# Retention's and GLA's q and k projected for all four heads at once

## The chip, the cores and the metric

One NeuronCore of a Trainium2 chip runs the whole program as one launch. The metric is the device time of one execution in microseconds. The time before is 2238.5 us, the median of three runs (2236.98 to 2249.15).

## The reference, cut to what matters

One layer of a hybrid decoder for 256 prompt tokens and 8 x 4 sample tokens, 288 tokens in all, width 2048, float32:

```
h = rmsnorm(x);  P = h @ w_in            # one projection, columns split among the mixers
retention (4 heads, dk 128, dv 256): rotary q, k; chunked recurrence; group norm; swish gate
gated DeltaNet "GDN" (8 heads, 128 x 128): conv + SiLU on q, k, v; delta rule; gated norm
GLA (4 heads, dk 128, dv 256): per-channel forget gate; chunked recurrence; gated norm
merge = sum_i sigmoid(P_gate_i) * (branch_i @ w_branch[i]);  x += merge @ w_o
x += SwiGLU(rmsnorm(x));  y = rmsnorm(x)
outputs: y and the new states of every head, for the prompt and for each sample row
```

The columns of `w_in` hold, among others, retention's q (512 columns, 128 per head), its k (512), its v (1024) and its gate (1024), and the same four for GLA.

## The kernel before, in words

Every product is taken in three parts: an activation is split into a high and a low float32r half (`xh`, `xl`), a weight likewise (`wh`, `wl`), and TensorE adds wh*xh, wh*xl and wl*xh into PSUM. Each weight tile is therefore loaded (`raw`, 512 KB, four buffers), cast by ScalarE (`wh`) and subtracted by VectorE (`wl`), with four buffers of each, before TensorE uses it. The weights stand still in TensorE and the 288 tokens stream through.

Two routines do this for the mixers. `products` (L405, called by `x_in`) takes 256 columns at a time and loads four blocks of 128 rows per tile, so that a row of a transfer has 256 columns; L422 and L423 are its cast and subtraction. `halves` (L337, called by `x_halves`) takes 512 columns, loads two blocks of rows per tile and works through the two halves of the columns in turn, with four PSUM accumulators (`pd`); its cast is at L355. With `perm`, which rotary needs, the cast reads even and odd columns apart.

The mixers' stage is a loop of four turns (L1457). Each turn first projects a pair of GDN heads (`gdn`: q, k, v with a short convolution, and a gate `sz`, four calls of `x_in`), then a pair of retention heads (first two turns) or of GLA heads (last two): q and k by `x_in`, two heads' v and gate by `x_halves` (`two_heads`). The heads' own work (scores, triangular solve, states, norms) is written as generators: `gdn_mix` for a pair of GDN heads, `ret_head` and `gla_head` for one wide head. A generator is started when its inputs are projected. `pump` is called after each pair of row blocks of a projection and steps every active generator by its rate, the GDN kind in one call and the others in the next, so that the heads' small instructions come in between the products in program order. A scheduler then orders each engine's queue in a simulated run, the older instruction first, with loads, casts and subtractions of weights ahead of the rest.

Buffers: `ev` (nine tiles of two heads x 288) holds projected q, k, v and gates; `s0` (three tiles of 4 KB per partition) holds the sample states, of which a GDN head takes one and a wide head two; `srow` (one) holds the old convolution rows of a GDN block and `ns` (one) the new ones on their way out. All these transfers are issued by SyncE (SP), in one queue with the weight loads. The GDN pool is freed when the last pair is done; the pool of the following branch stage (gates of the merge, branch products, `yr`, `bt`) is made after it and uses memory that it frees.

Of the kernel before, what the change touches and what calls it, by code (L numbers as in the profile page):

```python
# [10 lines left out]
F32 = mybir.dt.float32  # L11
F32R = mybir.dt.float32r
# [27 lines left out]
R1 = 4  # L40
R2 = 6
EV = 9
ORDER = (1, 2, 3, 0)

O_RQ, O_RK, O_RV, O_RG = 0, 512, 1024, 2048
O_GQ, O_GK, O_GV = 3072, 4096, 5120
# [55 lines left out]
class Trunk:  # L102
# [231 lines left out]
            evict(m, tiles[m][:, :T])  # L334
        return pool

    def halves(self, xh, xl, wv, kt, evict):  # L337


        nc, tc = self.nc, self.tc  # L340
        acc = [self.t(self.pd, (P, 512), "pd") for _ in range(4)]
        for k0 in range(0, kt, 4):
            raws = []
            for z in (k0, k0 + 2):
                raw = self.t(self.wp, (P, 2, WIDE), "raw", bufs=4)
                with tc.high_priority():
                    nc.sync.dma_start(out=raw, in_=wv[:, z:z + 2])
                raws.append(raw)
            for half in range(2):
                for z, raw in enumerate(raws):  # L350
                    wh = self.t(self.wp, (P, 2, CHUNK), "wh", F32R, bufs=4)
                    wl = self.t(self.wp, (P, 2, CHUNK), "wl", F32R, bufs=4)
                    src = raw[:, :, half * CHUNK:(half + 1) * CHUNK]
                    with tc.high_priority():
                        nc.scalar.copy(wh, src)  # L355
                        self.tt(wl, src, wh.bitcast(F32), ALU.subtract)
                    for k in range(2):
                        kk = k0 + 2 * z + k
                        for m in range(2):
                            ms = slice(m * P, (m + 1) * P)  # L360
                            o = acc[2 * half + m][:, :T]
                            self.mm(o, wh[:, k, ms], xh[kk], kk == 0, False)
                            self.mm(o, wh[:, k, ms], xl[kk], False, False)
                            self.mm(o, wl[:, k, ms], xh[kk], False, kk == kt - 1)
                        self.pump(k)
                if k0 + 4 == kt:
                    for m in range(2):
                        evict(2 * half + m, acc[2 * half + m][:, :T])

    def x_halves(self, c0, evict):  # L370
        self.halves(blocks(self.xh), blocks(self.xl), self.w_in(c0, WIDE), KT, evict)

    def products4(self, xh, xl, wv, kt, steps=None):
        nc, tc = self.nc, self.tc
# [179 lines left out]
    def gdn_conv(self, pair, part):  # L554

        nc, m = self.nc, self.mx
        c0 = part * 1024 + pair * CHUNK
        b0 = c0 // P
        cat = self.t(self.gd, (P, 2, CA), "cat", bufs=2)
        nc.vector.memset(cat[:, :, 0:3], 0.0)  # L560
        srow = self.t(self.gd, (24, CHUNK), "srow", bufs=1)
        nc.sync.dma_start(out=srow, in_=self.i["state_gdn_conv"][0].rearrange("b r c -> (b r) c")[:, c0:c0 + CHUNK])
        smp = [cat[:, mm_, 3 + NPR:CW].rearrange("p (b r) -> p b r", r=7) for mm_ in range(2)]
        out = self.t(m, (P, 2, T), "ev", bufs=EV)

        def ev(mm_, pp):
            self.tt(cat[:, mm_, 3:3 + NPR], pp[:, :NPR], self.rb[:, :NPR], ALU.mult)
            self.tt(smp[mm_][:, :, 3:7], pp[:, NPR:].rearrange("p (b t) -> p b t", t=NT),
                    self.rb[:, NPR:].rearrange("p (b t) -> p b t", t=NT), ALU.mult)

        self.x_in(O_GQ + c0, ev)
        pt = self.ps()
        for mm_ in range(2):
            self.tr(pt[:, 24 * mm_:24 * mm_ + 24], srow[:, mm_ * P:(mm_ + 1) * P])
# [12 lines left out]
        l3 = self.t(self.gd, (P, 2, 27), "l3", bufs=2)  # L587
        for mm_ in range(2):
            nc.vector.tensor_copy(l3[:, mm_].rearrange("p (b r) -> p b r", r=3),
                                  cat[:, mm_, NPR:NPR + 63].rearrange("p (b r) -> p b r", r=7)[:, :, 0:3])  # L590
        self.start(self.conv_state(l3, c0), 1, "conv")
        return out

    def conv_state(self, l3, c0):
        nc = self.nc
        yield
        yield
        pt = self.ps()
# [4 lines left out]
        nc.sync.dma_start(out=self.o["p_conv"][0, 0, :, c0:c0 + CHUNK], in_=ns[0:3])  # L603
        nc.sync.dma_start(out=self.o["s_conv"][0].rearrange("b r c -> (b r) c")[:, c0:c0 + CHUNK], in_=ns[3:27])

    def gated(self, n, c0):

# [43 lines left out]
    def gdn_mix(self, pair, qs, ks, vs, szs):  # L651
# [58 lines left out]
        for hh, z in enumerate(hd):  # L710
# [14 lines left out]
            dts = []  # L725
            for g, (t0, w) in enumerate(GROUPS):
                nmk = self.mats[:, MAT_NM] if g < 2 else self.small[:, SM_NM:SM_NM + 32]
                dt_ = big("dt", 3, w)
                self.stt(dt_, cb[:w, t0:t0 + w], gcol[:w, g, h:h + 1], nmk, ALU.subtract, ALU.add)
                self.act(dt_, dt_, AF.Exp)  # L730
                dts.append(dt_)
# [206 lines left out]

    def expand(self, v3, e, b0):
        n = 512 // e  # L940
        vx = self.t(self.mx, (3 * NS, 512), "vx", F32R, bufs=3)
        self.nc.gpsimd.tensor_tensor(vx.rearrange("p (b e) -> p b e", e=e), v3.unsqueeze(1).to_broadcast([3 * NS, n, e]),
                                     self.bmask[:, b0:b0 + n].unsqueeze(2).to_broadcast([3 * NS, n, e]), op=ALU.mult)
        return vx
# [13 lines left out]
    def gdn(self, pair):  # L958
# [3 lines left out]
            self.gates()  # L962
        v = self.gdn_conv(pair, 2)
        sz = self.gated(2, O_DZ + pair * CHUNK)
        self.start(self.gdn_mix(pair, q, k, v, sz), 1, "gdn")


    def values(self, v):
# [13 lines left out]
    def wide_head(self, h, st, st2, vt, vs, zq, kd, s0, state_out, p_out, decay, sg, gcols, n):  # L982
# [3 lines left out]

        def halves(b):
            sh = self.t(m, (P, 256), "sh", F32R, bufs=2)
            sl = self.t(m, (P, 256), "sl", F32R, bufs=4)
            src = s0[b // 4][:, b % 4]  # L990
            nc.scalar.copy(sh, src)
            nc.gpsimd.tensor_tensor(sl, src, sh.bitcast(F32), op=ALU.subtract)
# [81 lines left out]
            s0.append(s)  # L1074
        return s0

    def evict_scaled(self, c0, perm=False):
        out = self.t(self.mx, (P, 2, T), "ev", bufs=EV)

        def ev(m, pp):  # L1080
            self.tt(out[:, m], pp, self.rb, ALU.mult)

        self.x_in(c0, ev, perm)
        return out


    def rotated(self, c0):
        out = self.t(self.mx, (P, 2, T), "ev", bufs=EV)

        def ev(m, pp):  # L1090
            b = self.r1()
            self.tt(b[0:64], pp[64:128], self.rot[64:128, 1], ALU.mult)
            self.tt(b[64:128], pp[0:64], self.rot[0:64, 1], ALU.mult)
            self.tt(out[:, m], pp, self.rot[:, 0], ALU.mult)
            self.tt(out[:, m], out[:, m], b, ALU.add)

        self.x_in(c0, ev, perm=True)
        return out

    def spread(self, h, q, f):  # L1100
# [69 lines left out]
        yield from self.wide_head(h, st, st2, vt, vs, zq, kd, s0, s_out, p_out, lambda b: g4, sg, None, 0)  # L1170

    def ret(self, pair):
        q = self.rotated(O_RQ + pair * CHUNK)
        k = self.rotated(O_RK + pair * CHUNK)
        self.two_heads(O_RV + pair * WIDE, O_RG + pair * WIDE,
                       lambda hh, v, sg: self.ret_head(2 * pair + hh, q[:, hh], k[:, hh], v, sg), "ret")

# [99 lines left out]
    def gla(self, pair):  # L1277
        b = self.t(self.mx, (P, 2, T), "ev", bufs=EV)
        self.nc.sync.dma_start(out=b, in_=self.fsum[pair])
        q = self.t(self.mx, (P, 2, T), "ev", bufs=EV)  # L1280

        def evq(m, pp):
            self.stt(q[:, m], pp, DK ** -0.5, self.rb, ALU.mult, ALU.mult)

        self.x_in(O_LQ + pair * CHUNK, evq)
        k = self.evict_scaled(O_LK + pair * CHUNK)
        self.two_heads(O_LV + pair * WIDE, O_LG + pair * WIDE,
                       lambda hh, v, sg: self.gla_head(2 * pair + hh, q[:, hh], k[:, hh], v, sg, b[:, hh]), "gla")

# [159 lines left out]
    def run(self):  # L1449
# [4 lines left out]
        self.wd = self.pool("wide", stack=mst, side="right")  # L1454
        self.gd = self.pool("gdn", stack=dst, side="right")
        self.gdn_setup()
        for n, (f, pair) in enumerate(((self.ret, 1), (self.ret, 0), (self.gla, 1), (self.gla, 0))):  # L1457
            self.gdn(ORDER[n])
            if n == 0:
                self.wide_setup()  # L1460
# [66 lines left out]
```

## Time and profile before

| what | value |
|---|---|
| time, median of 3 runs | 2238.5 us |
| profiled execution | 2237.24 us, span 2235.4 us |
| TensorE matmul busy | 2170.1 us, 97% |
| VectorE, ScalarE, GpSimd busy | 1356.0, 1027.8, 213.5 us |
| HBM read, written | 341.70 MB, 25.69 MB |

A busy time counts an engine's instructions, not its waits. The clock column of a window is the share of TensorE's full clock that was granted there. A wait is put down to the instruction or transfer that ended it. The mixers' stage lasts from the start to about 765 us, the branch stage follows.

### The profile page before, as it was taken

The page shows a single profiled execution, that of the slowest core. Times are in us where ns is not written, and L with a number is a line of the kernel's source. Part 1 is how long each engine was busy: PE and PEld are TensorE (multiplying, and loading weights), DVE is VectorE, ACT ScalarE, POOL GpSimd, SP SyncE. Part 2 cuts the span into 40 slices and gives each one's busy share as a digit, 9 for nine tenths or more (in the row PEclk, how much of TensorE's full clock was granted, in tenths as well). Part 3 has the DMA queues.
Part 4 walks back from the last instruction along what each step waited for, and adds up shares of the span by engine and source line. Part 5 has one row for each costly group of instructions (what it writes and reads, how often), then busy time and mean ns, then how long its engine had stood idle before and what let it go on. Part 6 is the DMA issues. An engine that isn't in the chain of part 4 may idle for free.

```text
span 2235.4 us, 43857 instructions
## 1 busy us (share of the span) xinstructions
PE 2170.1 (97%) x17020; PEld 2113.2 (95%) x17020; DVE 1356.0 (61%) x2952; ACT 1027.8 (46%) x2114; POOL 213.5 (10%) x264
## 2 busy tenths in 40 slices
PE   8999989999989999999999999999999999999997
PEld 7899979989878999999999999999999999999997
DVE  6776765685777586555565655565555445556544
ACT  5645443453445355444444444444444334444443
POOL 2103301241233042000000000000000000000000
PEclk9999999999999999999999999999999999999998
DMA  8747876864997666677666566655555555555553
GB/s 221 160 127 164 148 161 121 192 176 124 132 114 189 125 192 199 190 194 186 175 187 168 163 191 179 179 167 167 164 169 163 169 164 167 167 164 169 161 160 118
DMA packets 251511, 370.23 MB, mean 166 GB/s; under 512 B 20318, under 2 KB 120248, under 8 KB 251144
## 3 DMA queue, kind: packets, MB, share of 16 engines
q1 hardware_dynamic: 250136, 364.66, 63.7%
q8 instruction: 133, 2.18, 0.4%
q0 software_dynamic: 896, 2.45, 0.3%
q14 instruction: 74, 0.61, 0.1%
q10 hardware_dynamic: 272, 0.34, 0.1%
HBM read 341.70 MB, written 25.69 MB: 164 GB/s over the span
## 4 chain that ended last, share of the span: by engine, by line
PE 87%; DMA 9%; DVE 2%; ACT 1%; issue 1%; POOL 0%; SPq 0%; POOLq 0%; DVEq 0%; ACTq 0%
PE pd L129 54%; PE pm L129 32%; DMA raw<-in_w_in_dram 4%; DMA yr<-ys 1%; PE pm L126 1%; DMA out_dram<-s 1%; DVE wl L135 1%; DMA srow<-in_state_gdn_conv_dram 1%; DVE r L144 0%; DMA ev<-fsum 0%; DMA s<-in_state_ret_dram 0%; DMA xa<-in_x_prompt_dram 0%; ACT wh L422 0%; DMA xb<-in_x_sample_dram 0%; DMA out_dram<-ns 0%
## 5 line engine op out<-in xcount | busy, mean ns | idle before, releaser
L135 DVE TENSOR_TENSOR wl<-raw,wh 128x512 fp32r<-128x512 f32 (+1 forms) x1208 | 846.2, 703 | 705.0 <-ACT wh L386 489.7
L129 PE MATMUL pd<-xh,wh 128*128 128x288 f32 x2768 | 824.4, 300 | 16.2 <-ACT wh L422 12.3
L129 PE MATMUL pd<-xl,wh 128*128 128x288 f32 x2768 | 824.5, 299 | 0.0
L129 PE MATMUL pd<-xh,wl 128*128 128x288 f32 x2768 | 816.9, 299 | 1.0 <-DVE wl L135 1.0
L386 ACT CAST wh<-raw 128x512 fp32r<-128x512 f32 x784 | 485.2, 620 | 643.9 <-PE pd L129 331.6
L129 PEld LDWEIGHTS pd<-xh,wh 128*128 128x128 f32 x2768 | 523.4, 189 | 21.8 <-ACT wh L422 13.1
L129 PEld LDWEIGHTS pd<-xl,wh 128*128 128x128 f32 x2768 | 524.2, 189 | 3.7 <-issue 1.6
L129 PEld LDWEIGHTS pd<-xh,wl 128*128 128x128 f32 x2768 | 520.5, 189 | 5.6 <-DVE wl L135 2.9
L355 ACT CAST wh<-raw 128x512 fp32r<-128x512 f32 x224 | 138.0, 618 | 194.3 <-PE pd L129 178.6
L129 PE MATMUL pm<-xh,wl 128*128 128x288 f32 x704 | 207.8, 295 | 0.0
L129 PE MATMUL pm<-xl,wh 128*128 128x288 f32 x704 | 207.3, 294 | 0.0
L129 PE MATMUL pm<-xh,wh 128*128 128x288 f32 x704 | 207.0, 294 | 0.0
L422 ACT CAST wh<-raw 128x512 fp32r<-128x512 f32 x192 | 117.8, 622 | 101.3 <-PE pd L129 52.9
L129 PEld LDWEIGHTS pm<-xh,wh 128*128 128x128 f32 x704 | 132.1, 188 | 0.0
L129 PEld LDWEIGHTS pm<-xl,wh 128*128 128x128 f32 x704 | 132.1, 188 | 0.0
L129 PEld LDWEIGHTS pm<-xh,wl 128*128 128x128 f32 x704 | 132.0, 188 | 0.0
L129 PE MATMUL pd<-ah,wl 128*128 128x288 f32 x352 | 103.9, 295 | 0.0
L129 PE MATMUL pm<-ah,wl 128*128 128x288 f32 x352 | 103.9, 295 | 0.0
L129 PE MATMUL pm<-al,wh 128*128 128x288 f32 x352 | 103.8, 295 | 0.0
L129 PE MATMUL pd<-al,wh 128*128 128x288 f32 x352 | 103.7, 295 | 0.0
L129 PE MATMUL pm<-ah,wh 128*128 128x288 f32 x352 | 103.7, 295 | 0.0
L129 PE MATMUL pd<-ah,wh 128*128 128x288 f32 x352 | 103.6, 294 | 0.0
(372 smaller groups left out, 2927.9 us busy)
## 6 DMA issues: line engine op xcount, KB each, us to landing
raw<-in_w_in_dram SPq DMA_DIRECT2D x252, 512.0 KB
raw<-in_w_gate_up_dram SPq DMA_DIRECT2D x176, 512.0 KB
raw<-in_w_down_dram SPq DMA_DIRECT2D x88, 512.0 KB
raw<-in_w_branch_dram SPq DMA_DIRECT2D x48, 512.0 KB
raw<-in_w_o_dram SPq DMA_DIRECT2D x32, 512.0 KB
out_dram<-s SPq DMA_DIRECT2D x16, 512.0 KB
s<-in_state_gdn_dram SPq DMA_DIRECT2D x8, 512.0 KB
s<-in_state_ret_dram SPq DMA_DIRECT2D x16, 256.0 KB
```

The source lines that it names most:

```text
L126: self.nc.tensor.transpose(out, in_, self.ident[:k, :k])
L129: self.nc.tensor.matmul(out, lhsT=lhsT, rhs=rhs, start=start, stop=stop)
L135: self.nc.vector.tensor_tensor(out, a, b, op=op)
L355: nc.scalar.copy(wh, src)
L386: nc.scalar.copy(wh, raw[:, k])
L422: nc.scalar.copy(h, src)
```

## The change

Retention and GLA project q and k of all four heads in the turn of pair 0, by `x_halves` in rows of 512 columns; pair 0's come into `ev` tiles, pair 1's into two new tiles `qk`, which pair 1's turn takes. So pair 0 comes first now, in both, and the order of the GDN pairs is another one. `halves` learns `perm`, with the cast and the subtraction of such a tile done in two pieces, one for each block of rows. Four kinds of buffers get one fewer (`l3`, `dt`, `vx`, `sl`). The load of `srow` and the two stores of `ns` are issued by ScalarE. The last GDN pair's generator is stepped twice per pump.

```diff
-ORDER = (1, 2, 3, 0)
+ORDER = (1, 0, 2, 3)
...
-    def halves(self, xh, xl, wv, kt, evict):
+    def halves(self, xh, xl, wv, kt, evict, perm=False):
...
+                    pieces = [(wh, wl, src)]
+                    if perm:
+                        src = src.rearrange("p k (h m two) -> p k h two m", two=2, h=2)
+                        h, l = (y.rearrange("p k (h two m) -> p k h two m", two=2, h=2) for y in (wh, wl))
+                        pieces = [(h[:, y], l[:, y], src[:, y]) for y in range(2)]
                     with tc.high_priority():
-                        nc.scalar.copy(wh, src)
-                        self.tt(wl, src, wh.bitcast(F32), ALU.subtract)
+                        for h, l, src in pieces:
+                            nc.scalar.copy(h, src)
+                            self.tt(l, src, h.bitcast(F32), ALU.subtract)
...
+    def both(self):
+        return self.t(self.mx, (P, 2, T), "ev", bufs=EV), self.t(self.mx, (P, 2, T), "qk", bufs=2)
...
-        nc.sync.dma_start(out=srow, in_=self.i["state_gdn_conv"][0]...)
+        nc.scalar.dma_start(out=srow, in_=self.i["state_gdn_conv"][0]...)
...
-        l3 = self.t(self.gd, (P, 2, 27), "l3", bufs=2)
+        l3 = self.t(self.gd, (P, 2, 27), "l3", bufs=1)
...
-        nc.sync.dma_start(out=self.o["p_conv"]..., in_=ns[0:3])
-        nc.sync.dma_start(out=self.o["s_conv"]..., in_=ns[3:27])
+        nc.scalar.dma_start(out=self.o["p_conv"]..., in_=ns[0:3])
+        nc.scalar.dma_start(out=self.o["s_conv"]..., in_=ns[3:27])
...
-                dt_ = big("dt", 3, w)
+                dt_ = big("dt", 2, w)
...
-        vx = self.t(self.mx, (3 * NS, 512), "vx", F32R, bufs=3)
+        vx = self.t(self.mx, (3 * NS, 512), "vx", F32R, bufs=2)
...
-        self.start(self.gdn_mix(pair, q, k, v, sz), 1, "gdn")
+        self.start(self.gdn_mix(pair, q, k, v, sz), 2 if pair == ORDER[-1] else 1, "gdn")
...
-            sl = self.t(m, (P, 256), "sl", F32R, bufs=4)
+            sl = self.t(m, (P, 256), "sl", F32R, bufs=3)
...
     def rotated(self, c0):
-        out = self.t(self.mx, (P, 2, T), "ev", bufs=EV)
+        out = self.both()
...
-        self.x_in(c0, ev, perm=True)
+        self.x_halves(c0, ev, perm=True)
...
     def ret(self, pair):
-        q = self.rotated(O_RQ + pair * CHUNK)
-        k = self.rotated(O_RK + pair * CHUNK)
+        if pair == 0:
+            self.qk = self.rotated(O_RQ), self.rotated(O_RK)
+        q, k = (z[pair] for z in self.qk)
...
     def gla(self, pair):
-        self.x_in(O_LQ + pair * CHUNK, evq)
-        k = self.evict_scaled(O_LK + pair * CHUNK)
+        if pair == 0:
+            qs = self.both()
...
+            self.x_halves(O_LQ, evq)
+            ks = self.both()
...
+            self.x_halves(O_LK, evk)
+            self.qk = qs, ks
+        q, k = (z[pair] for z in self.qk)
...
-        for n, (f, pair) in enumerate(((self.ret, 1), (self.ret, 0), (self.gla, 1), (self.gla, 0))):
+        for n, (f, pair) in enumerate(((self.ret, 0), (self.ret, 1), (self.gla, 0), (self.gla, 1))):
```

## Rows read from the trace of the kernel before

**Rows 1.** The page, part 1: busy us (share) x instructions of each engine.
```profile
PE 2170.1 (97%) x17020; PEld 2113.2 (95%) x17020; DVE 1356.0 (61%) x2952; ACT 1027.8 (46%) x2114; POOL 213.5 (10%) x264
```

**Rows 2.** The chain in order of time: start, us, what; one block of 512 columns.
```profile
1401.92 25.44 PE pm L129 x192
```

**Rows 3.** Windows of the mixer stages: busy us of each engine, clock, DMA share, GB/s.
```profile
core 0: us, PE busy (x) PEld busy (x) DVE busy (x) ACT busy (x) POOL busy (x), PEclk, DMA share, GB/s
...
50.00:75.00 25.00, 17.65 (x119) 16.91 (x118) 15.90 (x39) 10.32 (x24) 3.67 (x4) 0.86 0.90 190
...
275.00:300.00 25.00, 15.09 (x98) 13.62 (x96) 8.21 (x30) 8.71 (x32) 2.61 (x3) 0.90 0.86 187
300.00:325.00 25.00, 25.00 (x197) 23.86 (x196) 23.74 (x79) 13.23 (x32) 1.42 (x2) 0.90 0.61 125
...
475.00:500.00 25.00, 21.15 (x133) 19.07 (x132) 21.77 (x82) 14.90 (x53) 8.67 (x10) 0.80 0.70 210
...
575.00:650.00 75.00, 69.69 (x515) 64.76 (x514) 54.10 (x154) 34.53 (x89) 24.04 (x36) 0.98 1.01 139
650.00:675.00 25.00, 13.97 (x95) 12.72 (x94) 15.29 (x34) 8.45 (x24) 6.65 (x7) 0.84 0.86 137
```

**Rows 4.** The same view, four microseconds after a stall.
```profile
484.00:488.00 4.00, 4.00 (x18) 4.00 (x18) 3.79 (x24) 2.61 (x9) 1.01 (x1) 0.50 1.00 325
```

**Rows 5.** SP's queue in order of time: start, us of the issue, line, transfer.
```profile
50.56 0.41 SPq L562 DMA_DIRECT2D srow<-in_state_gdn_conv_dram  x1
```

**Rows 6.** TensorE in order of time: start, us, out<-in, [idle before <- what ended it].
```profile
5.29 0.20 PE L126 MATMUL pm<-ident,rm 16*128 16x16 f32 x1 [0.47 <-DMA rm<-in_norm_mix_dram]
...
58.58 0.41 PE L126 MATMUL pm<-ident,srow 24*128 24x24 f32 x2 [6.49 <-DMA srow<-in_state_gdn_conv_dram]
...
284.49 0.58 PE L129 MATMUL pd<-xh,wh 128*128 128x288 f32 x1 [4.50 <-ACT wh L422]
```

**Rows 7.** ScalarE in order of time, its queue of issues (ACTq) included.
```profile
1.20 0.45 ACTq L188 DMA_DIRECT2D rm<-in_norm_mix_dram  x1
...
283.53 0.36 ACT L602 COPY ns<-pm 27x256 f32<-27x256 f32 x1 [10.39 <-DMA out_dram<-ns]
...
673.06 0.71 ACT L991 CAST sh<-s 128x256 fp32r<-128x256 f32 x2 [11.79 <-DMA s<-in_state_gla_dram]
```

**Rows 8.** Waits of the whole span: who <- for whom: us, times, longest.
```profile
SPq L1073 <- DMA out_dram<-s: 50.9, 16, 13.1
...
ACT wh L422 <- DMA raw<-in_w_in_dram: 44.8, 18, 6.0
...
PE pm L129 <- ACT sh L991: 10.6, 1, 10.6
...
ACT wh L355 <- DMA raw<-in_w_in_dram: 7.3, 3, 3.0
```

**Rows 9.** The cast of 256 columns (ns min/median/max), and the page's row of subtractions.
```profile
L422 ACT CAST wh<-raw x192: 601/619/680, 8.7 to 700.1; 128x512 fp32r<-128x512 f32 x192
...
L135 DVE TENSOR_TENSOR wl<-raw,wh 128x512 fp32r<-128x512 f32 (+1 forms) x1208 | 846.2, 703 | 705.0 <-ACT wh L386 489.7
```

**Rows 10.** The last GDN pair and the first, in order of time (VectorE, TensorE, SP).
```profile
675.89 0.81 DVE L135 TENSOR_TENSOR ev<-pd,rb 128x288 f32<-128x288 f32 x2
...
708.77 0.40 PE L129 MATMUL pm<-chl,sel 40*128 40x288 f32 x1
...
805.26 0.94 DVE L144 SCALAR_TENSOR_TENSOR yo<-pm,cols,ev 128x288 f32<-128x288 f32 x2
805.42 0.80 SPq L1297 DMA_DIRECT2D yr<-ys  x2
...
815.94 0.45 DVE L135 TENSOR_TENSOR bt<-pd,rb 128x288 f32<-128x288 f32 x1
...
111.44 0.40 PE L129 MATMUL pm<-chl,sel 40*128 40x288 f32 x1
...
204.43 0.51 DVE L144 SCALAR_TENSOR_TENSOR yo<-pm,cols,ev 128x288 f32<-128x288 f32 x1
```

More of the change, by code (lines that the diff above doesn't have):

```diff
@@ L368, in halves, with x_halves @@
                         evict(2 * half + m, acc[2 * half + m][:, :T])
-    def x_halves(self, c0, evict):
-        self.halves(blocks(self.xh), blocks(self.xl), self.w_in(c0, WIDE), KT, evict)
+    def x_halves(self, c0, evict, perm=False):
+        self.halves(blocks(self.xh), blocks(self.xl), self.w_in(c0, WIDE), KT, evict, perm)
+    def both(self):
+        return self.t(self.mx, (P, 2, T), "ev", bufs=EV), self.t(self.mx, (P, 2, T), "qk", bufs=2)
     def products4(self, xh, xl, wv, kt, steps=None):
@@ L561, in gdn_conv @@
         srow = self.t(self.gd, (24, CHUNK), "srow", bufs=1)
-        nc.sync.dma_start(out=srow, in_=self.i["state_gdn_conv"][0].rearrange("b r c -> (b r) c")[:, c0:c0 + CHUNK])
+        nc.scalar.dma_start(out=srow, in_=self.i["state_gdn_conv"][0].rearrange("b r c -> (b r) c")[:, c0:c0 + CHUNK])
         smp = [cat[:, mm_, 3 + NPR:CW].rearrange("p (b r) -> p b r", r=7) for mm_ in range(2)]
@@ L602, in conv_state @@
         nc.scalar.copy(ns, pt[:27, :CHUNK])
-        nc.sync.dma_start(out=self.o["p_conv"][0, 0, :, c0:c0 + CHUNK], in_=ns[0:3])
-        nc.sync.dma_start(out=self.o["s_conv"][0].rearrange("b r c -> (b r) c")[:, c0:c0 + CHUNK], in_=ns[3:27])
+        nc.scalar.dma_start(out=self.o["p_conv"][0, 0, :, c0:c0 + CHUNK], in_=ns[0:3])
+        nc.scalar.dma_start(out=self.o["s_conv"][0].rearrange("b r c -> (b r) c")[:, c0:c0 + CHUNK], in_=ns[3:27])
     def gated(self, n, c0):
@@ L1075, in wide_state @@
         return s0
-    def evict_scaled(self, c0, perm=False):
-        out = self.t(self.mx, (P, 2, T), "ev", bufs=EV)
[L1080 to L1084, printed above, removed]
     def rotated(self, c0):
-        out = self.t(self.mx, (P, 2, T), "ev", bufs=EV)
+        out = self.both()
         def ev(m, pp):
             b = self.r1()
+            o = out[m // 2][:, m % 2]
             self.tt(b[0:64], pp[64:128], self.rot[64:128, 1], ALU.mult)
             self.tt(b[64:128], pp[0:64], self.rot[0:64, 1], ALU.mult)
-            self.tt(out[:, m], pp, self.rot[:, 0], ALU.mult)
-            self.tt(out[:, m], out[:, m], b, ALU.add)
-        self.x_in(c0, ev, perm=True)
+            self.tt(o, pp, self.rot[:, 0], ALU.mult)
+            self.tt(o, o, b, ALU.add)
+        self.x_halves(c0, ev, perm=True)
         return out
@@ L1279, in gla, with evq, evk @@
         self.nc.sync.dma_start(out=b, in_=self.fsum[pair])
-        q = self.t(self.mx, (P, 2, T), "ev", bufs=EV)
-        def evq(m, pp):
-            self.stt(q[:, m], pp, DK ** -0.5, self.rb, ALU.mult, ALU.mult)
-        self.x_in(O_LQ + pair * CHUNK, evq)
-        k = self.evict_scaled(O_LK + pair * CHUNK)
+        if pair == 0:
+            qs = self.both()
+            def evq(m, pp):
+                self.stt(qs[m // 2][:, m % 2], pp, DK ** -0.5, self.rb, ALU.mult, ALU.mult)
+            self.x_halves(O_LQ, evq)
+            ks = self.both()
+            def evk(m, pp):
+                self.tt(ks[m // 2][:, m % 2], pp, self.rb, ALU.mult)
+            self.x_halves(O_LK, evk)
+            self.qk = qs, ks
+        q, k = (z[pair] for z in self.qk)
         self.two_heads(O_LV + pair * WIDE, O_LG + pair * WIDE,
```

## The prediction

> **What bounds the kernel now.** I read the page's busy times first, then the span cut into stages, then who waits for whom, then the time-ordered lists around the longest waits. TensorE is busy for 2170.1 of 2235.4 us [rows 1]: its work bounds the kernel, and the change keeps every product. A block of 96 products (256 columns of weights, sixteen blocks of rows, hi and lo parts) costs 12.7 us (192 take 25.44 [rows 2]). Retention's and GLA's q and k are eight such blocks before and after, 102 us both times. At stake is only what TensorE idles or runs slowly, and that lies in the mixer stages [rows 3]: idle are 7.35 us from 50 to 75 us, 9.9 from 275 to 300, 3.85 from 475 to 500, 5.3 from 575 to 650 and 11.0 from 650 to 675, in all 37 of the 65 us that the span holds. After a long stall the granted clock is at its lower level (0.50, 1.2 of 2.4 GHz): 18 recorded products in 4 us [rows 4], 0.22 us each, where the upper level gives 0.13 [rows 2]. A stretch loses its length times one minus its clock: 3.5, 2.5, 2.5, 5.0, 1.5 and 4.0 us in the six rows, 19 us, a quarter of it in time that was idle anyway. So the rows hold 37 + 14 = 51 us, 2.3% of the span, and that is the ceiling of a gain.
>
> The stalls have three roots. (a) Small transfers wait behind 512 KB weight loads on SP's one queue: the 24 KB of `srow` are issued at 50.56 us [rows 5], and the transpose that needs them starts at 58.58 after 6.49 us idle [rows 6]; ScalarE's copy to `ns` at 283.53 waits 10.39 us for the previous `ns` to leave [rows 7]. (b) State tiles: `s0` has three buffers, a pair of GDN heads holds two, and a wide head (retention, GLA) wants two. SP stands 50.9 us in 16 pieces, 13.1 the longest, until a state is written out and the next may be loaded [rows 8]; ScalarE stands 11.79 us at 673.06 at the cast of a state that isn't there [rows 7], and TensorE 10.6 with it [rows 8]. (c) Weight rows of 256 columns: ScalarE waits for weights 44.8 us in 18 pieces at L422, which casts 192 tiles [rows 8, 9], but 7.3 in 3 at L355 [rows 8], which casts rows of 512 (partly in the branch stage, where less else is moved).
>
> **The change part by part.**
> *Loads.* An x_in call loads four tiles of 512 KB, an x_halves call eight: 32 loads for q and k before and after, the same bytes in rows twice as long. The stretch with the DMA full (share 1.01) has 5.3 us idle and 1.5 of clock [rows 3]. Gain 0 to 7 us; I take 5, because the L355 row is the nearest.
> *Casts.* For retention's four blocks a cast of 512 elements (619 ns, perm or not [rows 9]) becomes two of 256, and so does the subtraction (703 ns [rows 9]). A half costs at least half and at most all of it: 32 casts more, 0 to 20 us on ScalarE, 0 to 22 on VectorE. Both lie under the twelve products (1.6 us) that use them, on engines busy for 46% and 61% [rows 1]. I take 0. Without that cover a third of it could show (the stretches with VectorE above 80%), 7 us, which I keep for the range.
> *`srow` on ScalarE's queue.* It takes away up to 6.49 us and the slow time after it (3.5 us [rows 3]): 0 to 10. The nearest row for the new way is `rm`, 8 KB issued by ScalarE at 1.20 us [rows 7] with 256 KB just ahead of it on SP, and used at 5.29 after a wait [rows 6]: 4.1 us to landing in place of `srow`'s 8.0. By that 3.9 of the 6.5 go, and a stall of 2.6 us may not lower the clock: I take 7. What is queued behind the issue on ScalarE are its weight casts, with up to four tiles (6 us of products) made ahead; the buffer that the issue waits for is freed by transposes directly after the block before. Late next is the weight load that shares the DMA with it.
> *`ns` on ScalarE's queue.* Copy and issues then stand on one engine, and no issue waits behind others on SP. Of the 10.39 us TensorE lost 4.50 [rows 6], and half of the clock's loss in the two stretches there, 2.5 [rows 3]. Bounds 0 and 10 (a part of the 3.85 at 475 may belong to the next `ns`); I take 7, both terms. The 36 issues cost ScalarE about the 0.41 us that `srow`'s takes on SP [rows 5], 15 us in all, hidden in its 54% idle time; uncovered they would be 15 us, for the range.
>
> The Trainium skill speaks against both: "DMA: Bandwidth & Descriptors", section "Issuing engines are not separate DMA queues", says that transfers started by different engines share the same DMA engines and that another issuer saves only the time to issue. By it the two gains would be about nothing, and the sum 14 us worse; the trace's one row, `rm`, lies between a landing at once and one as late as now, and doesn't settle it.
>
> *Held tiles and the order of pairs.* The generators of the heads are stepped once per pair of row blocks that the products pass. A GDN pair has 40 steps, 5 blocks of products. Stages held 10 blocks each (four of GDN, q, k, two of v, two of gate); now they hold 12, 8, 12 and 8. In stages 1 and 3 the GDN states are written before the first wide head asks for its own; in 2 and 4 the value block follows the GDN blocks at once, and the heads ask while the GDN pair holds two buffers. What state waits cost now is the 10.6 us at 673 with its clock (3 us outside the stall), the other half of the stalls from 275 to 325 (5.4 and 2.5), and the 3.85 and 5.0 us from 475 to 500: 30 us. The meeting of the two heads of a pair, where the second wants what the first writes out, stays, but falls where rows of 512 are loaded. Bounds: all 30 gone, and 10 worse (one more stall like that at 673, in stage 2). I take -10, a third: the mechanism stays, its places change. Held past the pair are only q and k; nothing waits for their two buffers, since GLA's come a whole stage after retention's last use.
> *The end of the last stage.* The branch stage's tiles lie in memory that the GDN pool frees: its first load is issued at 805.42 us, and the last GDN outputs are formed at 805.26 [rows 10]. Until then the first gate block stays in its four accumulators, the last of which is evicted at 815.94 [rows 10], and TensorE can't go past it. Now TensorE arrives there at about that time. From the last GDN projection (evicted at 675.89 [rows 10]) to 815.94 it had 140 us of work; 25.4 of them, q and k, leave the stage, so 115 remain. The GDN chain took 129 us (to 805.26), 97 of them after its second head's matmul at 708.77; the same part took 93 in stage 1 (111.44 to 204.43 [rows 10]), where no other heads run beside it. So it is bound by its own latency, and rate 2 shortens the first 33 us at most. Starving is 129 - 115 = 14 us, less up to 15 that rate 2 and emptier engines give back, or more by a stall like that at 673: bounds 0 and 35. I take +9, with the clock.
> *Buffers and ORDER.* `sl` waits one more step for a product, `vx`, `dt` and `l3` delay late GDN steps; they lie beside products, which hide them. ORDER changes which heads a stage computes and nothing of their size. Bounds 0 and 8 (half a microsecond for each of some 16 steps); I take +3.
>
> Sum: -5 - 7 - 7 - 10 + 9 + 3 = -17 us. The profiled execution took 2237.24 us (span 2235.4 and 1.8 around it): 2220. The runs' median is 1.3 us above that execution: 2221.5.
>
> **Rivals.**
> 1. *The last GDN pair starves TensorE.* The chain is held up by two GLA heads that now run later, and the state stalls move without going: +35 for +9, 0 for -10: 2221.5 + 26 + 10 = 2257. It decides from the point where the chain behind the last GDN projection is longer than some 130 us, when nothing else is left to run. For it: TensorE and the chain already arrive together at 805. Against: rate 2, and the 93 us of the undisturbed part.
> 2. *A small transfer is as late from ScalarE's queue*, because the backlog sits in the shared DMA engines: the gains of 7 and 7 are gone, 2235, no change. For it: a DMA share of 0.86 to 0.90 around both waits [rows 3]. Against: `rm`'s 4.1 us. (This is what the section of the Trainium skill above would make of it.)
> 3. *The stalls move and none of the state's goes*, and rows of 512 wait as the others did, so that the change doesn't do what it says: -7 - 7 + 9 + 3 = -2, 2236, no change.
> 4. *All meetings go*: -7 - 10 - 10 - 25 + 3 = -49, 2189.
>
> **How the numbers follow.** The forecast, 2200 to 2233 by its own terms, gets 0.49, rival 1 0.14, rival 2 0.12, rival 3 0.14, rival 4 0.11. A measurement can tell 0.5%, 11 us, from no change. Faster than 2227: rival 4, 0.42 of the forecast and 0.05 of rivals 2 and 3, so 0.58. Slower than 2250: 0.12 of rival 1, and 0.02 of rivals 2 and 3 with uncovered casts and issues: 0.14. Between: 0.28. The range from 2193 to 2248 leaves out most of rival 1 and half of rival 4.
>
> **What would show it.** Right: no TensorE wait for `srow`; ScalarE's waits for `ns` under 1 us each; hardly a wait for raw at the perm casts; TensorE idle for under 25 us up to 700 us; a gap of 5 to 15 us before the first `yr` load. Wrong: `srow` lands 8 us after its issue (rival 2); a gap of over 25 us before the first `yr` load (rival 1); ScalarE standing over 10 us for a retention state in stage 2 (rival 3).

## Result and the profile after

The change made the kernel slower. In eleven runs of each the median is 2257.86 us against 2243.83 before (2238.5 was the median of the first three), a ratio of 1.0071 with a 95% interval from 1.0058 to 1.0085. The prediction was 2221.5 us (2193 to 2248): wrong in sign, and outside its range. The profiled execution has a span of 2253.5 us, 18.1 more than the 2235.4 of before. TensorE is as full as it was, 97% [rows 1], with 14.5 us more of busy time for the same 17020 products; a busy time includes time at the lower clock. Its idle time grew only from 65.3 to 68.9 us, while the mean granted clock fell from 0.986 to 0.982: most of the loss is work done more slowly after a stall, and less of it is more idle time.

Page of the changed kernel, part 1:

```profile
PE 2184.6 (97%) x17020; PEld 2122.3 (94%) x17020; DVE 1358.5 (60%) x2984; ACT 1034.5 (46%) x2146; POOL 199.8 (9%) x264
```

The windows of the mixer stages, columns as in [rows 3] (the last one lies in the branch stage):

```profile
225.00:250.00 25.00, 23.72 (x167) 21.60 (x166) 14.66 (x34) 11.62 (x25) 6.85 (x7) 1.00 1.00 98
250.00:275.00 25.00, 17.79 (x99) 16.48 (x99) 12.78 (x32) 9.25 (x26) 5.14 (x6) 0.80 0.84 149
275.00:300.00 25.00, 21.79 (x146) 18.66 (x144) 14.80 (x46) 10.90 (x25) 6.42 (x7) 1.00 1.02 125
300.00:325.00 25.00, 19.79 (x126) 17.90 (x126) 12.09 (x32) 6.54 (x13) 0.00 (x0) 0.93 0.91 189
325.00:350.00 25.00, 18.23 (x115) 17.28 (x113) 13.71 (x51) 13.75 (x46) 4.06 (x4) 0.80 0.47 144
...
475.00:500.00 25.00, 20.41 (x118) 16.94 (x118) 22.33 (x55) 13.99 (x38) 10.22 (x11) 0.86 0.60 134
500.00:525.00 25.00, 19.37 (x116) 16.18 (x115) 16.39 (x66) 13.22 (x51) 7.26 (x8) 0.80 0.57 152
575.00:650.00 75.00, 75.00 (x572) 71.14 (x571) 48.79 (x129) 34.01 (x82) 17.06 (x27) 1.00 0.76 163
650.00:675.00 25.00, 25.00 (x185) 23.37 (x184) 20.76 (x52) 14.32 (x35) 11.61 (x15) 1.00 0.53 110
...
812.00:838.00 26.00, 23.94 (x163) 21.35 (x162) 22.07 (x72) 12.85 (x36) 10.83 (x19) 0.87 0.67 209
```

Read the second column (TensorE busy) against the length, and the clock (third from the end). Turn 4, which idled 16.3 us from 575 to 675 before [rows 3], now idles not at all. Turn 2 pays for it: from 250 to 350 us 22.4 us are idle (10.8 before), and the clock costs another 11.75 us (0.20, 0.00, 0.07 and 0.20 of 25 us each; part of that falls in the idle time; 5.0 before). Another 10.2 idle and 8.5 of clock stand between 475 and 525 (3.85 and 5.0 before). So the stalls moved to the middle, and those of the middle grew. Note the last two columns of turn 2: the DMA is full (1.00, 1.02) while it moves 98 and 125 GB/s. That pair, a full DMA at a low rate, is what the kernel before showed from 575 to 650 (1.01 at 139) [rows 3]. It moved with the idle time.

Who waits in turn 2: the weight casts of ScalarE, in order of time, and then a head's state:

```profile
304.23 0.62 ACT L432 CAST wh<-raw 128x512 fp32r<-128x512 f32 x1 [5.33 <-DMA raw<-in_w_in_dram]
...
309.65 0.62 ACT L432 CAST wh<-raw 128x512 fp32r<-128x512 f32 x1 [4.29 <-DMA raw<-in_w_in_dram]
...
315.18 0.62 ACT L432 CAST wh<-raw 128x512 fp32r<-128x512 f32 x1 [3.94 <-DMA raw<-in_w_in_dram]
...
329.38 0.71 ACT L1001 CAST sh<-s 128x256 fp32r<-128x256 f32 x2 [8.11 <-DMA s<-in_state_ret_dram]
```

The whole span's waits (L432, L361 and L1001 were L422, L355 and L991):

```profile
ACT wh L432 <- DMA raw<-in_w_in_dram: 36.4, 12, 5.3
...
ACT sh L1001 <- DMA s<-in_state_ret_dram: 18.6, 3, 8.1
...
ACT wh L361 <- DMA raw<-in_w_in_dram: 11.1, 4, 3.6
```

The casts of 256 columns are 128 in place of 192, yet they wait 36.4 us in place of 44.8 [rows 8]; nearly the same wait falls on fewer tiles.

### The profile page after: what moved, and what is told of

The parts are those of the page before. It is cut to its first block, busy times and chain, and to the rows that moved or that the text cites. A ratio compares the mean times of both kernels' runs of the same rounds, so it can differ in the third digit from the quotient of the medians.

```text
span 2253.5 us, 43938 instructions
## 1 busy us (share of the span) xinstructions
PE 2184.6 (97%) x17020; PEld 2122.3 (94%) x17020; DVE 1358.5 (60%) x2984; ACT 1034.5 (46%) x2146; POOL 199.8 (9%) x264
## 3 DMA queue, kind: packets, MB, share of 16 engines
q0 software_dynamic: 896, 2.45, 0.3%
## 4 chain that ended last, share of the span: by engine, by line
PE 89%; DMA 7%; DVE 1%; ACT 1%; issue 1%; SPq 0%; POOL 0%; POOLq 0%; DVEq 0%; ACTq 0%
PE pd L129 56%; PE pm L129 32%; DMA raw<-in_w_in_dram 3%; PE pm L126 1%; DMA ys<-yo 1%; DMA yr<-ys 1%; DMA out_dram<-s 1%; DMA s<-in_state_ret_dram 1%; DVE wl L135 0%; DMA xa<-in_x_prompt_dram 0%; DMA s<-in_state_gla_dram 0%; DMA srow<-in_state_gdn_conv_dram 0%; DMA bmask<-in_c_bmask_dram 0%; POOL sl L1002 0%; ACT wh L432 0%
## 5 line engine op out<-in xcount | busy, mean ns | idle before, releaser
L135 DVE TENSOR_TENSOR wl<-raw,wh 128x512 fp32r<-128x512 f32 (+2 forms) x1240 | 847.1, 687 | 710.9 <-ACT wh L396 489.7
L396 ACT CAST wh<-raw 128x512 fp32r<-128x512 f32 x784 | 485.3, 620 | 644.5 <-PE pd L129 333.5
L129 PEld LDWEIGHTS pd<-xh,wh 128*128 128x128 f32 x2768 | 525.8, 190 | 27.1 <-issue 8.4
L361 ACT CAST wh<-raw 128x512 fp32r<-128x512 f32 (+1 forms) x320 | 180.8, 578 | 233.1 <-PE pd L129 215.1
L432 ACT CAST wh<-raw 128x512 fp32r<-128x512 f32 x128 | 78.0, 617 | 109.3 <-PE pd L129 53.3
```

The costliest lines, as they stand in the source:

```text
L129: self.nc.tensor.matmul(out, lhsT=lhsT, rhs=rhs, start=start, stop=stop)
L135: self.nc.vector.tensor_tensor(out, a, b, op=op)
L361: nc.scalar.copy(h, src)
L396: nc.scalar.copy(wh, raw[:, k])
L432: nc.scalar.copy(h, src)
```

## Experiments

Each ratio is to the kernel before, from runs taken in turn with it, with its 95% interval. e9 was executed once.

### Is it the joining?

e1 and e2 undo the joining in retention or in GLA alone; e11 is the kernel before with every part of the change but the joining.

```
e1  ret():  q, k = self.rotated(O_RQ + pair * CHUNK), self.rotated(O_RK + pair * CHUNK)   # by x_in
e2  gla():  self.x_in(O_LQ + pair * CHUNK, evq); k = self.evict_scaled(O_LK + pair * CHUNK)
e11 before + ORDER, order of pairs, ScalarE's issues, fewer buffers, rate 2
```

> The changed kernel with retention's q and k projected pair by pair in rows of 256 again; GLA's stay joined, all else stays. Theory 'places' (joining retention moves the state exchange of the wide heads so that it meets the GDN blocks of turns 2 and 3, where the changed kernel idles 33 us between 225 and 525 us against 15 before, while GLA's joining freed turn 4): the idle time of turns 2 and 3 falls back to some 15 us, turn 4 stays free; about 0.993 of the kernel before (2228). Theory 'queue' (ScalarE's issues of small transfers are what costs): no gain, 1.007. Theory 'tail' (the last GDN pair starves TensorE): no gain, since GLA's last turn stays short: 1.005 to 1.008.

> The changed kernel with GLA's q and k pair by pair again, retention's joined, all else as changed. 'Places': turns 2 and 3 keep their stalls and turn 4 gets its 18 us back: 1.010 to 1.014 of the kernel before. 'Tail': the last turn has its 25 us of q and k again, so the 5 us around 820 go: 1.003 to 1.005. 'Queue': 1.007.

> Everything of the change except the joining: the fewer buffers, both orders, the small transfers on ScalarE, rate 2 in the last turn; q and k pair by pair in rows of 256. The parts measured one at a time were 0 (buffers), 0 (small transfers) and +6 us (orders): if they add up, 1.003 of the kernel before, and the joining is worth the other 10 us. If the parts hinder each other: 1.007, and the joining costs nothing.

Measured: 1.0080 [1.0059, 1.0101], 1.0061 [1.0047, 1.0076] and 1.0081 [1.0058, 1.0103], against 1.0071 [1.0058, 1.0085] for the change. All overlap. Whatever the joining costs or gives is at most some tenths of a per cent, and the loss is there without it, in the other parts. The theory 'places' (0.993 for e1) is out.

### Is it the small transfers, the buffers or the rate?

```
e3  after:  nc.scalar.dma_start -> nc.sync.dma_start   for srow and both stores of ns
e4  before: nc.sync.dma_start -> nc.scalar.dma_start   for the same three
e5  before: l3 2 -> 1, dt 3 -> 2, vx 3 -> 2, sl 4 -> 3 buffers
e7  after:  self.start(self.gdn_mix(...), 1, "gdn")     for the last pair too
e8  after:  the four kinds of buffers as before, EV 9 -> 7
```

> The changed kernel with srow and ns issued by SP again. My prediction had the move at -14 us: undone, the time rises to about 1.013 of the kernel before. The rule that issuing engines are not separate queues: no difference, 1.007. 'Queue' as the cause of the loss: at or under 1.002.

> The kernel before with nothing changed but srow and ns issued by ScalarE. My prediction: -14 us, 0.994. The rule that issuing engines are not separate queues: 1.000. 'Queue' as the cause of the loss: 1.004 or more.

> The kernel before with the four kinds of buffers one fewer (l3 1, dt 2, vx 2, sl 3), nothing else. Theory 'buffers' (the fewer sl and vx let TensorE and ScalarE stand at the states' products, which all three variants of the changed kernel share): 1.005 to 1.008 of the kernel before, waits for sl and sh as in those. Theory 'order' (the pairs' and ORDER's new sequence costs): 1.000. My prediction had +3 us: 1.001.

> The changed kernel with the last GDN pair stepped once per pump, as the others. Theory 'tail' (the last GDN chain ends too late): the first load of yr, at 827 us now, comes later and TensorE idles longer there; 1.010 or more of the kernel before. Theory 'rate' (the second step crowds the engines and costs): 1.003. If the chain is bound by its own latency: no change, 1.007.

> The changed kernel with l3, dt, vx and sl at their old numbers, and seven in place of nine ev tiles to make room (eight aren't enough). 'Buffers': the stalls at sh and sl in turns 2 and 3 go; 0.998 to 1.002 of the kernel before, if the two ev tiles cost nothing. 'Order' or 'joining': 1.007 or more.

Measured: e3 1.0062 [1.0043, 1.0081], e4 0.9999 [0.9986, 1.0013], e5 0.9993 [0.9983, 1.0004], e7 1.0091 [1.0076, 1.0106], e8 1.0095 [1.0079, 1.0111]. None recovers the loss, and neither of the two tried alone in the kernel before (e4, e5) makes it. Rate 2 may help by 0.2% (the intervals overlap). e8 had to give up two `ev` tiles for room, so it doesn't tell what the buffers alone do with the new order; e16 below does.

e4 shows why the small transfers were worth nothing. Its queue on ScalarE, then TensorE:

```profile
55.81 0.30 ACTq L562 DMA_DIRECT2D srow<-in_state_gdn_conv_dram  x1
```

```profile
67.43 0.38 PE L126 MATMUL pm<-ident,srow 24*128 24x24 f32 x2 [9.83 <-DMA srow<-in_state_gdn_conv_dram]
```

This is the third block's `srow`. The second block's, whose transpose waited 6.49 us before [rows 6], is now issued at 45.51 and used at 50.18 without a wait; the third's, issued on a queue where no weight load stands ahead of it, is used 11.6 us later, where SP's queue had it used 7.5 us after its issue (59.43 to 66.97). So the wait moved on by one block. In the changed kernel the third block's load, issued at 55.68, is used at 60.44 after 2.45 us, and e3, which undoes only the move to ScalarE, waits 10.0 us in all for `srow`, yet takes the same time. In e4 the DMA share is 0.76 to 1.13 in every 2 us from 56 to 66: these 24 KB are late while the shared DMA engines are busy with other transfers, whichever queue they were issued on. This is the rule of the Trainium skill, "DMA: Bandwidth & Descriptors", section "Issuing engines are not separate DMA queues", that the prediction weighed; the runs agree with it (0.9999).

### Is it the order?

```
e6  before: ORDER = (1, 0, 2, 3), and pair 0 before pair 1 in retention and GLA; nothing else
e10 after:  ORDER = (1, 2, 3, 0); nothing else
```

> The kernel before with ORDER (1, 0, 2, 3) and pair 0 ahead of pair 1 in both mixers, nothing else. 'Order': 1.005 to 1.008. 'Buffers': 1.000. 'Joining' (that either q and k pair of calls is joined shifts v ahead against the GDN states): 1.000.

> The changed kernel with the GDN pairs in the old order (1, 2, 3, 0), all else as changed. 'Columns': pair 0's slow loads move from turn 2, where states are exchanged, to turn 4; the 22 us of idle time from 250 to 340 fall under 10, turn 4 gains under 10; 1.000 to 1.004 of the kernel before. 'Joining' as the only cause: 1.007.

Measured: e6 1.0027 [1.0015, 1.0039], e10 1.0002 [0.9989, 1.0014]. One constant takes the whole loss out of the changed kernel. Two windows of e6, where nothing but the order differs from before (its profiled execution took 2247.45 us, its median 2239.98):

```profile
275.00:300.00 25.00, 23.01 (x149) 21.66 (x150) 14.24 (x39) 11.30 (x25) 6.92 (x8) 0.86 0.98 146
...
575.00:650.00 75.00, 75.00 (x589) 70.05 (x588) 54.49 (x157) 35.59 (x92) 23.59 (x33) 1.00 0.64 142
```

The full DMA at a low rate is in turn 2 (0.98 at 146), and turn 4 is free of it, as in the changed kernel. It goes where GDN pair 0 goes: to turn 2 by (1, 0, 2, 3), to turn 4 by (1, 2, 3, 0); e10 has it back there, 1.00 at 100 from 600 to 625.

### Why the order matters

Pair 0 has the same work as the others but other columns of `w_in`. e9 measures the columns alone: it loads ranges of 256 columns (2048 rows, 2 MB, in four tiles of four row blocks as L325 does) and then ranges of 512, with a mark after each; it computes nothing and writes zeros.

```
for n, (c0, w) in enumerate(OFFS):
    ...
    for k0 in range(0, KT, kn):
        raw = pool.tile([P, kn, w], F32, ..., bufs=4)
        ...
        nc.sync.dma_start(out=raw, in_=src)
        nc.vector.tensor_copy(acc[:, 0:1], raw[:, 0, 0:1])
    nc.scalar.copy(acc[:, 1:2], acc[:, 0:1])
```

> No mixer work at all: the same transfers as in the kernel (512 KB, rows of 256 or 512 columns of w_in) one range of columns after another, with four buffers and nothing else on the queue; all results are left out (zeros are written). Theory 'columns' (the 1 KB pieces of GDN pair 0's columns, 3072, 4096, 5120 on, come half as fast wherever they are loaded, as 130 to 170 ns a piece against 75 to 85 in both traces): a range of 256 columns that starts at 3072 or 5120 takes some 1.5 to 2 times as long as those 256 to 768 columns further. Theory 'traffic' (they are slow only because state transfers run beside them): all ranges of 256 columns take the same time within 10%.

The marks, on ScalarE. The difference of two starts is the time of one range, as nearly as four buffers allow (the first tiles of a range are under way while the last of the one before land). These rows end the ranges that start at columns 3840, 4096, 4352, 4608, 4864, 5120 and 5376; then, after three not shown, the one at 3200 and those of 512 columns at 0, 512, 1024 and 1536. The first three ranges (3072, 3328 and 3584: 26.7, 27.1 and 35.0 us) ran beside the stores of zeros and tell nothing:

```profile
100.14 0.19 ACT L120 COPY acc<-acc 128x1 f32<-128x1 f32 x1 [11.21 <-DVE acc L119]
120.28 0.19 ACT L120 COPY acc<-acc 128x1 f32<-128x1 f32 x1 [19.96 <-DVE acc L119]
133.75 0.19 ACT L120 COPY acc<-acc 128x1 f32<-128x1 f32 x1 [13.28 <-DVE acc L119]
142.21 0.19 ACT L120 COPY acc<-acc 128x1 f32<-128x1 f32 x1 [8.26 <-DVE acc L119]
151.75 0.19 ACT L120 COPY acc<-acc 128x1 f32<-128x1 f32 x1 [9.35 <-DVE acc L119]
171.92 0.19 ACT L120 COPY acc<-acc 128x1 f32<-128x1 f32 x1 [19.98 <-DVE acc L119]
186.31 0.19 ACT L120 COPY acc<-acc 128x1 f32<-128x1 f32 x1 [14.20 <-DVE acc L119]
...
253.52 0.19 ACT L120 COPY acc<-acc 128x1 f32<-128x1 f32 x1 [13.23 <-DVE acc L119]
274.15 0.19 ACT L120 COPY acc<-acc 128x1 f32<-128x1 f32 x1 [20.45 <-DVE acc L119]
286.28 0.19 ACT L120 COPY acc<-acc 128x1 f32<-128x1 f32 x1 [11.94 <-DVE acc L119]
308.79 0.19 ACT L120 COPY acc<-acc 128x1 f32<-128x1 f32 x1 [22.32 <-DVE acc L119]
321.25 0.19 ACT L120 COPY acc<-acc 128x1 f32<-128x1 f32 x1 [12.26 <-DVE acc L119]
```

The same 2 MB take 20.1 us at 4096 and 20.2 at 5120 (pair 0's k and v, 104 GB/s), 13.5 and 14.4 for pair 1, 8.5 for pair 2 (248 GB/s), 9.5 for pair 3. A block of products takes 12.7 us [rows 2]. So pair 0's blocks can't be loaded as fast as TensorE uses them, even with the DMA to themselves, and pair 1's not quite. In bytes, pair 0's columns begin at 0 modulo 4096 in a row (at 64 for its gate, column 6160, measured 19.5 us), the others 1024, 2048 and 3072 further; a row has 65664 bytes. Ranges of 512 columns (4 MB, 25.4 us of products) take 20.6 us at 0, 12.1 at 512, 22.5 at 1024 and 12.5 at 1536.

Pair 0's columns are not the only ones at such an offset. In the kernel before, the DMA is also full at a low rate from 265 to 275 us (1.01 at 86 GB/s), and the weights that SP issues from 256.8 to 267.9 are those of retention pair 0's q, from column 0. The stores of `ns` that ScalarE waits 10.39 us for at 283.53 [rows 7] are issued behind them, at 268.36 and 274.48. The longest wait for `ns` is 10.9 us in e13 below, where these loads stay, and 3.3 in e6, where retention's pairs change places as in the change and these loads go to turn 1: that wait, too, probably has slow columns at its root.

e12 takes the addresses away from the changed kernel, and e13 from the kernel before: GDN pair 0 projects pair 3's columns in place of its own (its heads' results differ), with the same instructions in the same order.

```
self.x_in(O_GQ + c0 + (768 if pair == 0 else 0), ev)
sz = self.gated(2, O_DZ + (pair or 3) * CHUNK)
```

> The changed kernel with the GDN pair 0's q, k, v and gate projected from pair 3's columns (those results are pair 3's): the same bytes and instructions at other addresses. 'Columns': pieces of 80 ns in turn 2, its idle time from 225 to 340 falls by half or more, and the time by 10 to 18 us: 0.999 to 1.003 of the kernel before. 'Traffic' or 'joining': no change, 1.007.

> The kernel before with GDN pair 0 reading pair 3's columns of w_in (those heads' results differ). Theory (pair 0's own columns load at about 100 GB/s instead of 150 to 250, whatever turn they stand in): the stretch from 575 to 675 us, where pair 0 is projected, loses most of its 16 us idle and part of 5.5 us of clock: 2220 to 2230, ratio 0.990 to 0.995. Rival (the loss of the change lay in which heads meet in turn 2, and columns matter there alone): no change, 0.998 to 1.002.

Measured: e12 0.9933 [0.9913, 0.9952], e13 0.9940 [0.9919, 0.9961]. The addresses alone cost the changed kernel 1.4% (1.0071 to 0.9933, some 31 us) and the kernel before 0.6% (13 us). With quick columns for pair 0 the two kernels take the same time, as far as the intervals tell: the whole loss of the change hangs on these addresses. The windows of e12 beside those of the changed kernel above:

```profile
225.00:250.00 25.00, 25.00 (x181) 23.29 (x180) 18.59 (x47) 14.38 (x31) 6.16 (x7) 1.00 0.77 167
250.00:275.00 25.00, 25.00 (x182) 23.29 (x182) 23.27 (x52) 15.98 (x40) 10.63 (x11) 1.00 0.82 194
275.00:300.00 25.00, 24.20 (x180) 23.37 (x179) 18.11 (x46) 10.30 (x20) 4.17 (x4) 1.00 0.78 218
300.00:325.00 25.00, 24.09 (x182) 23.01 (x183) 20.34 (x76) 15.82 (x51) 3.03 (x2) 1.00 0.46 145
```

The 98 to 149 GB/s at shares of 0.84 to 1.02 are 167 to 218 at 0.77 to 0.82 from 225 to 300. By the traces' records of single packets, the pieces of 1 KB, most of them weights, take 168 ns on average from 225 to 250 us in the changed kernel and 77 in e12: such a piece holds a DMA engine more than twice as long. The granted clock stays at 1.00, its upper level of 2.4 GHz. SP's issues of the twelve weight tiles of k, v and gate (L325; first and last start behind the durations in ns), of the changed kernel and of e12:

```profile
L325 SPq DMA_DIRECT2D raw<-in_w_in_dram x12: 368/698/4732, 226.9 to 304.7; - x12
```

```profile
L325 SPq DMA_DIRECT2D raw<-in_w_in_dram x12: 368/375/792, 227.4 to 276.7; - x12
```

They go out over 78 us with the slow columns and over 49 with the quick ones. And the wait of the casts of 256 columns, in e12 and in e13:

```profile
ACT wh L432 <- DMA raw<-in_w_in_dram: 7.9, 4, 3.9
```

```profile
ACT wh L422 <- DMA raw<-in_w_in_dram: 11.5, 6, 4.7
```

They were 36.4 and 44.8 [rows 8]: most of what the prediction called stall root (c) was one pair's addresses, not the length of the rows in general.

### What is left, and what can be done

e16 is e11 with every buffer as before, so that it and e6, e11 and the change form a ladder.

```
e16 before + ORDER, order of pairs, ScalarE's issues, rate 2; buffers as before
e15 e10 + the wide heads' sample states loaded and stored by nc.gpsimd.dma_start
```

> The kernel before with the new ORDER and order of pairs, the small transfers on ScalarE's queue and rate 2 for the last GDN pair, but every buffer as before (the order alone gave 1.0027, all of it but the joining 1.0081). If the fewer buffers cost only with the new order, this is near the order alone: 1.001 to 1.004, 2242 to 2248 us. If they cost nothing there either, 1.006 to 1.010 remains, and it is the small transfers or the rate beside the new order.

> The kernel after with the old ORDER (1, 2, 3, 0), and the sample states loaded and stored through GpSimd's queue instead of SyncE's. The old ORDER alone gave 1.0002. If SyncE's queue, standing at a state load until a buffer is written out, holds weight loads back, the stalls of 2 to 7 us at the states go: 2225 to 2235, ratio 0.992 to 0.998. If the slow columns and the shared transfers are what is left, nothing changes: 0.999 to 1.002. GpSimd's own work behind a waiting issue could make it worse: 1.003 or more.

Measured: e16 1.0038 [1.0022, 1.0053]. The ladder: order alone 1.0027, with the small transfers and the rate 1.0038, with fewer buffers 1.0081, with the joining 1.0071. The fewer buffers, free in the old order (0.9993), cost some 0.4% in the new one. Which of the four wasn't tried. e15, with the states of the wide heads on GpSimd's queue, gave 0.9996 [0.9982, 1.0010], as e10 did: taking them off SP's queue gains nothing when pair 0 is last.

e14 was meant to place pair 0's blocks between retention's wide ones, in turn 1, where no head's states are moved from 60 to 180 us.

```
ORDER = (0, 1, 2, 3)
def gdn(self, pair):
    if pair == 0: rq = self.rotated(O_RQ)
    q = self.gdn_conv(pair, 0)
    if pair == 0: self.qk = rq, self.rotated(O_RK)
    k = self.gdn_conv(pair, 1)
```

> The kernel after with GDN pair 0 in turn 1, its q and k projected between retention's two wide blocks (order: retention q, pair 0's q, retention k, pair 0's k, v, gate). Theory (slow loads show only where several follow one another; a wide block of 25.4 us of products loads in 12 to 21 us and lets the buffers fill again): most of the 27.5 us idle and 13.7 us of clock in the stretch from 250 to 450 us goes, and two slow blocks (v, gate) cost up to 15 us in turn 1: 2220 to 2238, ratio 0.990 to 0.998. Rival (turn 2's waits come from the states of turn 1's heads): they stay, 1.004 to 1.010.

Measured: 1.0178 [1.0158, 1.0198], the worst of all. Its expectation had the order wrong: the first pair's q is projected in the set-up already (L257), so pair 0's k, v and gate followed one another after both wide blocks. Spreading was therefore not tested; what the run shows is that turn 1 is no better place. Two windows of e14:

```profile
100.00:125.00 25.00, 20.48 (x144) 19.14 (x143) 15.23 (x35) 6.13 (x13) 0.00 (x0) 1.00 0.79 67
125.00:150.00 25.00, 16.75 (x99) 14.42 (x98) 11.96 (x36) 6.70 (x16) 0.00 (x0) 0.90 0.98 92
```

No state is moved there, and the weights still come at 67 and 92 GB/s (in the first window beside twelve narrow loads for the gates). The states of other heads, my rival for turn 2, aren't needed for the slow rate. Why the same slow loads cost least in the last turn and most in the first wasn't separated.

e18 joins what loads slowly: q and k of GDN pairs 0 and 1, in rows of 512. e17 is its control at the same order.

```
e17 before: ORDER = (2, 3, 0, 1); dt 3 -> 2, vx 3 -> 2, sl 4 -> 3
e18 e17 +
+    def gdn_conv2(self, part):
+        rows = [self.gdn_rows(pair, part, pair == 0) for pair in range(2)]
+        evs = [self.gdn_evict(cat) for cat, _ in rows]
+        self.x_halves(O_GQ + part * 1024, lambda m, pp: evs[m // 2](m % 2, pp))
+        rows[1] = rows[1][0], self.gdn_srow(part * 1024 + CHUNK, self.r2()[:24, :CHUNK])
...
+        if pair == 0:
+            self.gq = self.gdn_conv2(0), self.gdn_conv2(1)
```

> The kernel before with ORDER (2, 3, 0, 1) and fewer buffers of dt, vx and sl (these without the new order cost nothing, 0.9993); it is the control of the next run. Theory: pair 0's slow loads move from turn 4 to turn 3, beside GLA's heads instead of retention's: 0.999 to 1.004. Rival (any order that takes pair 0 out of the last turn pays as the change does): 1.005 to 1.010.

> The same with q and k of GDN pairs 0 and 1 projected together in rows of 512 columns in pair 0's turn (pair 1's held in two tiles, the old convolution rows of pair 1 loaded into a scratch tile). Theory: alone, a range of 512 columns at the slow offset loads in 21 to 22.5 us, 10.5 to 11.3 us for each 12.7 us of products, so two of pair 0's four slow blocks no longer hold TensorE up; half of the price that the columns had in the kernel before (0.6%) goes: 0.994 to 0.998. Rival (rows of 512 help no more here than for retention and GLA, where joining gave at most 0.1%; or two convolutions in a row and the late old rows take it back): the control's time to 0.2%.

Measured: e17 1.0063 [1.0042, 1.0084], e18 0.9997 [0.9982, 1.0012]. The control is slower than the theory's 0.999 to 1.004, as its rival had it: of the orders tried, only pair 0 in the last turn costs no more than before. e18 misses its 0.994 to 0.998, and its rival, the control's time, as well. Joining the slow pair gives 0.7% against the control, where joining retention and GLA gave nothing that could be measured. Casts of 256 columns waiting for weights, e17 and e18:

```profile
ACT wh L422 <- DMA raw<-in_w_in_dram: 53.2, 16, 6.4
```

```profile
ACT wh L422 <- DMA raw<-in_w_in_dram: 9.0, 5, 4.0
```

It still doesn't beat the kernel before. One loss is in its own trace, the old rows of pair 1, which it asks for late:

```profile
483.75 0.41 PE L126 MATMUL pm<-ident,r 24*128 24x24 f32 x2 [12.09 <-DMA r<-in_state_gdn_conv_dram]
```

A version with these rows loaded ahead, or with v and gate joined too, was not tried. Of the versions that compute everything, none is faster than the kernel before by more than the measurement tells.

## Why the prediction was wrong

- **The step that failed** is "ORDER changes which heads a stage computes and nothing of their size", in the +3 for buffers and ORDER. Size is not all that a block of weights has; its addresses set how fast it loads. With the rest of the change in place, ORDER is worth 0.69% (1.0071 against 1.0002 in e10), about 15 us, where I had bounded it at 8 together with the buffers; alone in the kernel before, with the wide pairs' order, it is 0.27% (e6), and the fewer buffers add some 0.4% in that order (e11 against e16). The sign was in the rows: 1.01 of the DMA at 139 GB/s from 575 to 650, beside 0.86 at 187 from 275 to 300 [rows 3]. I read the full DMA as a matter of row length and didn't ask why it moved less while fuller.
- **`srow` and `ns`, -14**: nothing (e3, e4). Rival 2 was right for these terms: `ns` still waits 5.5 us once, and `srow` 2.4, against 15.3 and 7.3 before, but the time didn't follow. Taking a wait off one instruction took no work off the DMA engines.
- **State meetings, -10**: they moved and none went, as rival 3 said. ScalarE waits 18.6 us for retention's states, in three pieces (8.11 at 329, 8.06 at 445), and 7.5 for GLA's, 26.1 in all; before it waited 21.0 us in all for states, 11.79 of them at 673 [rows 7]. How much of these waits is itself due to the slow loads just ahead wasn't separated.
- **Loads in rows of 512, -5**: not shown. e11 against the change allows a gain of 0.1%, with intervals that also allow none. Retention's q, at column 0, still loads for 20.6 us in rows of 512, its k for 12.1; the casts of rows of 512 wait 11.1 us for weights (7.3 before [rows 8]), none of it worth naming at retention's q and k. And stall root (c), which the term came from, was the columns' place more than the length of the rows: 44.8 us of it became 11.5 in e13.
- **Casts, 0**: in the changed kernel half a cast takes 422 ns and half a subtraction 415; e1, which takes these halves back, gains nothing that shows. Right.
- **The end of the last stage, +9**: the mechanism was there and smaller. TensorE doesn't idle from 700 to 812 us; from 812 to 838 it idles 2.06 us at a clock of 0.87, some 5 us in all, where before it didn't idle and had its full clock. Rival 1, 35 us there, didn't happen, and that its 2257 us meets the 2257.86 measured is chance; turn 4 had become free of stalls, and rate 2 was worth at most some 0.2%.
- **Range and chances.** All my terms were stalls of the kernel before, each priced as if the others stood still; no rival let the largest, the slow stretch of turn 4, come back larger elsewhere.

What stays open: why these addresses are slow, and why they cost more in turn 2 (1.4%) than in turn 4 (0.6%). The runs show dependence on the column's offset, no more. The Trainium skill, "DMA: Bandwidth & Descriptors", section "Latency and other measured facts", has a related measurement: copies between HBM tensors whose row pitch per partition is a large power of two slow down, to 207 GB/s at 512 KiB, 164 at 2 MiB and 103 at 4 and 8 MiB, against 214 with 4 KiB of padding and 97 with 192 bytes; it calls its mechanism an inference. Here the pitch is 64 KiB and 128 bytes and no run varied it, so whether the 104 GB/s against 248 have the same cause isn't shown.

## What to carry to other kernels

Before reordering blocks that look alike, read the DMA share and the GB/s of each one's stretch together: a stretch that is full at a low rate may belong to its data's addresses, as here, and then moves with them. Measure the loads alone, one range after another; it is one short run. And ask of a wait that is to be taken away whether what it waits for gets less to do: moving `srow` and `ns` to another queue left the DMA engines the same work, and the time stayed.

## What the hardware showed unexpectedly

Loading 256 of 16416 float32 columns over 2048 rows takes 8.5 to 20.2 us by the start column alone: 20.1 and 20.2 us at byte offset 0 modulo 4096, 13.5 and 14.4 at 1024, 8.5 at 2048, 9.5 and 11.4 at 3072; and 13.4 at 512, pair 0's columns moved by 128. With 512 columns it is 20.6 to 22.5 us at offset 0 (2048 rows, 4 MB) and 12.1 to 12.5 at 2048 (by the six ranges of retention's columns, where slow and quick took turns). The range at 3840 (11.4 us) followed those that ran beside the stores of zeros and is the least sure. All this is from one execution of e9; e12 and e13 bear out offset 0 against 3072 in whole kernels.
